# Three joints of a seven-product trunk put into written order, and a kernel's last loads reordered

## The chip, the cores and the metric

One core of one Trainium2 chip runs the whole program, in one launch. The time is device microseconds (us) of that core, the median of the runs; lower is better. The engines are named as the profile names them: PE (TensorE, matmuls), PEld (its weight loads), DVE (VectorE), ACT (ScalarE), POOL (GpSimd), and SP (SyncE), which here only issues transfers. PE's clock has two levels, 1.2 and 2.4 GHz; the profile gives the granted share of the upper one.

## The reference

A trunk of two layers over x of 1024 positions by 1024 channels, in float32, each followed by a squared-ReLU MLP with 4096 hidden channels. Cut to what matters here:

```python
# layer 0: chunked spatial gating (SGU)
z = gelu(rmsnorm(x, g) @ w_in + b_in);  u, v = split(z)          # 2 x 2048 channels
v = layernorm(v);  s = einsum('gij,bnjgc->bnigc', w_s * mask, v) + b_s
x = x + (u * s) @ w_out
x = x + square(relu(rmsnorm(x, g) @ ffn_w1[0])) @ ffn_w2[0]      # 1024 -> 4096 -> 1024
# layer 1: RWKV-7 time mixing, then
x = x + y @ w_o
x = x + square(relu(rmsnorm(x, g) @ ffn_w1[1])) @ ffn_w2[1]
out = rmsnorm(x, final_norm_g)
```

## The kernel before, in words

Every float32 operand is split into a high part, cast to fp32r by ACT, and a low part, the rest, subtracted by DVE or POOL (`tt`, L327). Each product is three matmuls (high-high L160, low-high L161, high-low L162), each of 128 x 128 weights by 512 columns.

**Seven-product stages.** The gate's product x @ w_in[:, :2048] with its w_out, and the two MLPs, are made by `two_products` (L425). It cuts each matrix product into 2 x 2 blocks and computes it with seven block products M1 to M7 instead of eight. The left sides are A11, A12, A22 and the sums S1 to S4; the right sides are B11 to B22 and sums T1 to T4, which POOL makes (`weights`, L460). The first half, the *ups*, runs over pairs p of 128-column blocks of w1 and over M1, M5, M6, M2, M7, M3, M4 in each; one such product is 12 matmuls. `prepare(n)` (L487) loads, sums, casts and splits the weights of product n, six products ahead; `evict` (L540) turns the PSUM banks upa to upd into blocks y0 to y3, squares them and stores them to DRAM (zd). The second half, the *down* (from L612), computes these blocks times w2, in chains of 12 matmuls into banks dnu, dnv, dnw, in the order M1, M5, M6, M7, M4, M3, M2, four chains q to a step, and DVE adds each chain to the residual tiles xd0 to xd7. A *unit* u is half a step's operands: a stored block zr and a weight block w2B, each cast by ACT and split by DVE into the four tiles op... (`prepare_z` L685, `prepare_w` L697). `LAST_UNITS` (L624) says in which memory the last six units lie.

**Norm between stages.** `Spread` (L334) takes each finished residual tile t of 128 positions: `scale` (L360) squares and sums it on ACT, takes a root on ACT (rs), refines the reciprocal root on DVE (five small instructions, L243 to L252), and DVE scales it (sn, L368). `transpose` (L370) makes eight PE transposes into two banks st, and from them the split parts of A22 and S1 (t below 4), or of A11, A12, S2, S3 and S4 (t from 4 on). So a full set of left sides stands only after the last tile. There are two of these, f0 behind the gate's down and f1 behind the rwkv's last product wo.

**What sets the order.** A scheduler orders the instructions of PE, DVE, ACT and POOL by its own estimates, except inside `tc.manual_schedule`, where the named engines keep the written order: the last 14 products of the ups and the down up to its last three steps (L772). Each engine then runs its list strictly in order, and SP issues transfers in order on one queue. The rwkv part in between is not touched.

Three kinds of joint come up below: into the ups of a stage (the gate's behind the v products, the MLPs' behind the gate's down and behind wo), and from the ups to the down of the same stage (in all three stages).

Of the kernel before, what the change touches and what calls it, by code (L numbers as in the profile page):

```python
# [12 lines left out]
F32 = mybir.dt.float32  # L13
# [108 lines left out]
def trunk(ctx: ExitStack, tc: tile.TileContext, a: dict, out: bass.AP):  # L122
# [211 lines left out]
    class Spread:  # L334


        def __init__(self, xs, g, tag, lag):
            self.xs, self.tag, self.lag = xs, tag, lag
# [4 lines left out]
            self.side, self.raw, self.wait = {}, [], []  # L343
            self.spilled = [dq.tile([P, 1024], F32, name=f"xm{tag}_{t}") for t in range(NT)]

        def open(self, name, where):
# [8 lines left out]
        def put(self, name, q, x, eng):  # L355
            hi, lo = [v[:, :, q * P : (q + 1) * P] for v in self.side[name]]
# [13 lines left out]
        def transpose(self, t):  # L370
            xn, q = self.xns[t % 3], t % 4
            o = []
            for j in range(2):
                o.append(pt(f"st{t}{j}_{self.tag}").rearrange("p (k n) -> p k n", k=4))
# [4 lines left out]
            if t < 4:  # L379
                if t == 0:  # L380
                    self.open("A22", 0)
                    self.open("S1", 1)
# [6 lines left out]
            else:  # L389
                if t == 4:  # L390
                    self.open("A11", (0, 1))
                    self.open("A12", (2, 3))
                    self.open("S2", 2)
                    self.open("S3", 3)
                    self.open("S4", (6, 7))
# [18 lines left out]
        def tick(self):  # L414
            for w in self.wait:
                w[1] += 1
            if self.wait and self.wait[0][1] >= self.lag:
                self.transpose(self.wait.pop(0)[0])
# [6 lines left out]
    def two_products(i, sides, w1, w2, residual, after_factory, gate=None):  # L425
# [9 lines left out]

        def load_pair(p):
            tags = (("raw0", "raw1"), ("wh0", "wl0"))[p % 2]
# [14 lines left out]
        if gate:  # L452
            gate.ws = ta[:, HB:].rearrange("p (s e i) -> p s e i", s=2, e=2)
            gate.open(0)
# [29 lines left out]
        ring = ("wh1", "wl1", "wh3", "wl3", "wh2", "wl2")  # L484
# [55 lines left out]
        def evict(m, p):  # L540

            if not ys:
                ys.extend(xt(j, f"y{j}_{i}").rearrange("p (e n) -> p e n", e=2) for j in range(4))
                u12.extend(tp.tile([P, HB], F32, tag=t, name=f"{t}_{i}") for t in ("tu", "td"))
            y1, y2, s13, s24 = ys
            u1, u2 = u12
            todo, held[:] = list(held), []
# [19 lines left out]
            if m == "M1":  # L567
                nc.scalar.copy(out=u1, in_=bank("a", p))
                if gate:
                    gate.open(p + 1)  # L570
# [9 lines left out]
            elif m == "M7":  # L580
# [8 lines left out]
                if gate:  # L589
                    gate.mix(p, "C22", s13[:, 1])  # L590
# [30 lines left out]
        raws, w12 = ("raw0", "raw1", "wh0", "wl0"), ("wh1", "wl1", "wh2", "wl2")  # L621
        if gate:
            UNITS = [raws, "h2", "h3", w12, "h1", "h0"]
            LAST_UNITS = ["h0", "h1", "h2", ("z2", "z3"), "h3", ("z6", "z7")]  # L624
        else:
            UNITS = [raws, "h2", "h1", "h3", "h0", w12]
            LAST_UNITS = ["h1", "h3", ("z2", "z3"), ("wh3", "wl3", "wh2", "wl2"), "h2", ("ta", "tb", "wh1", "wl1")]
# [45 lines left out]
        def side_b(u):  # L673

            gr, m = steps[u // 2]
            b = {kind: wr[gr, kind][:, 2 * (u % 2) : 2 * (u % 2) + 2] for kind in ("B11", "B12", "B21", "B22")}
# [62 lines left out]
        def up(first, last):  # L739
            for n in range(first, last):  # L740
# [4 lines left out]
                if early and 1 <= n <= 2:  # L745
                    sides.flush()
                for w in meanwhile.get(n - len(seq), ()):
# [6 lines left out]
        if gate:  # L754
            meanwhile = {
                -6: [lambda: load_z(0), lambda: load_z(1), lambda: load_w(0, ("B11", "B12"))],
                -5: [lambda: load_w(0, ("B22", "B21"))],
# [3 lines left out]
        else:  # L761
# [3 lines left out]
                -4: [lambda: load_w(0, ("B22", "B21")), lambda: unit(0)],  # L765
                -3: [lambda: unit(1)],
            }
        for n in range(6):
            prepare(n)
        ready = len(seq) - 14  # L770
        up(0, ready)
        with tc.manual_schedule(engines={ET.PE, ET.DVE, ET.Activation, ET.SP}):  # L772
# [3 lines left out]
            load_x(range(4))  # L776
            load_w(1, ("B12", "B11"))
            unit(2)
            unit(3)
            for n in range(len(steps) - 3):  # L780
                for q in range(4):
# [3 lines left out]
                    out()  # L785
# [6 lines left out]
        for q in range(4):  # L792
            chain(n, q)()
            (prepare_w if q % 2 else prepare_z)(2 * n + q // 2 + 4)
            after(q)
            tick()
        for q in range(4):
            chain(n + 1, q)()
            tick()
            if hasattr(after, "half"):  # L800
                after.half(4 + q)
            chain(n + 2, q)()
            after(4 + q)
            tick()
        return xs


    def sgu(norm, x, load_x, after_factory):
# [26 lines left out]
        st = sp.tile([P, NT, 8, 6], F32, name="vstat", bufs=1)  # L835

# [96 lines left out]


# [43 lines left out]
        with tc.manual_schedule(engines={ET.PE, ET.DVE, ET.Activation, ET.SP}):  # L978
            for c in range(2, 8):
# [5 lines left out]
                for t in range(NT):  # L985
# [3 lines left out]
                    if t > 1:  # L989
                        v_stat(c, t - 2)  # L990
                    if 0 < t < 3 and c < 7:
                        stream.ahead()
                    if sums and t > 4:
                        sums.pop(0)()
                    if (c, t) == (2, 2):
# [19 lines left out]

        mv = sp.tile([P, NT, 2], F32, name="vmv", bufs=1)
        for t in range(NT):
            nc.vector.bn_aggr(out=mv[:, t, :], in_=st[:, t, :, :])
        rstd = sp.tile([P, NT], F32, name="vrstd", bufs=1)
        nmr = sp.tile([P, NT], F32, name="vnmr", bufs=1)  # L1020
        nc.scalar.activation(out=rstd, in_=mv[:, :, 1], func=AF.Sqrt, bias=eps_t[LN_EPS])
        rstd = rsqrt_refine(rstd, mv[:, :, 1], NT, "v", 1.0, LN_EPS)
        nc.vector.scalar_tensor_tensor(
            out=nmr, in0=mv[:, :, 0], scalar=-1.0, in1=rstd, op0=ALU.mult, op1=ALU.mult
        )

        sums_close()

        class Gate:


            def __init__(self):
                self.v, self.taken = {}, {}

            def open(self, p):
                if p >= E // 256:
                    return
                if not p:
                    self.mixing(0)
                vt = self.v[p] = [  # L1040
                    xt(4 + 2 * (p % 2) + hf, f"vn{p}{hf}").rearrange("p (n c) -> p n c", n=4) for hf in range(2)
                ]
                for hf in range(2):
# [1139 lines left out]
```

## Time and profile before

| | us |
|---|---|
| runs (three) | 2683.47, 2692.83, 2696.07 |
| median | 2692.83 |
| profiled execution | 2697.68 |
| its span, first to last instruction | 2696.0 |
| mean granted PE clock | 0.979 |
| PE busy / DVE / ACT / POOL | 2563.1 / 1976.7 / 1049.8 / 720.4 |

The stages stand in the span at about: norm and v products 0 to 206, the gate's ups 206 to 403 and down 403 to 547, the MLP 0 ups 547 to 931 and down to 1155, rwkv to 1980, wo to 2051, the MLP 1 ups 2051 to 2386 and down to 2686. Busy time is a mean over all of these. In a fully used stretch of 50 us PE is busy for 50.00; what a joint loses is read from the gaps of PE there and from the stretch behind a gap in which the granted clock is at its lower level.

### The profile page before, as it was taken

How to read it: one execution, taken by the hardware profiler on the slowest of the kernel's cores; microseconds unless marked ns; L12 is line 12 of the kernel's file. 1: busy time of each engine (PE TensorE's matmuls, PEld its weight loads, DVE VectorE, ACT ScalarE, POOL GpSimd, SP SyncE). 2: the span in 40 equal slices, each digit the busy share in tenths (PEclk: the TensorE clock that was granted, in tenths of full speed). 3: DMA queues.
4: the chain of work that ended last, by engine and by line, in shares of the span. 5: the costliest groups of instructions: out<-in, count | busy, mean ns of one | idle time of the engine just before them, and what ended most of it. 6: DMA issues, size and time to landing. Idle time of an engine off the chain costs nothing. (4 is left out here: it accounts for less than half of the span.)

```text
span 2696.0 us, 41800 instructions
## 1 busy us (share of the span) xinstructions
PE 2563.1 (95%) x16202; PEld 2169.1 (80%) x16202; DVE 1976.7 (73%) x3011; ACT 1049.8 (39%) x1725; POOL 720.4 (27%) x545
## 2 busy tenths in 40 slices
PE   8999998989999999999999999977898999999998
PEld 8997887868888788877677898967877888878887
DVE  6448768787766887776676547999688766687777
ACT  4235434353333433345553322324425333343334
POOL 2243210143332000013464413244425333200002
PEclk9999999999999999999999999989899999999999
DMA  5424557335443744333577854444743644384332
GB/s 192 169 94 142 175 202 260 111 114 188 152 149 129 283 157 141 125 117 94 178 175 179 212 157 119 115 97 102 193 157 113 201 139 160 117 299 154 129 125 94
DMA packets 342616, 418.71 MB, mean 155 GB/s; under 512 B 91561, under 2 KB 238097, under 8 KB 342417
## 3 DMA queue, kind: packets, MB, share of 16 engines
q1 hardware_dynamic: 340208, 409.41, 48.5%
q0 software_dynamic: 2064, 6.36, 0.7%
q8 instruction: 127, 2.08, 0.3%
q14 instruction: 73, 0.59, 0.1%
q10 hardware_dynamic: 144, 0.26, 0.0%
HBM read 277.48 MB, written 138.48 MB: 154 GB/s over the span
## 5 line engine op out<-in xcount | busy, mean ns | idle before, releaser
L327 DVE TENSOR_TENSOR w1s<-w1r,w1s 128x512 fp32r<-128x512 f32 x120 | 128.5, 1072 | 72.1 <-ACT w1s L331 71.8
L161 PE MATMUL dnu<-oph 128*128 128x512 f32 x416 | 162.8, 391 | 0.9 <-DVE oph L327 0.9
L160 PE MATMUL dnu<-oph 128*128 128x512 f32 x416 | 163.6, 393 | 0.0
L162 PE MATMUL dnu<-oph 128*128 128x512 f32 x416 | 163.3, 392 | 0.0
L327 DVE TENSOR_TENSOR xd<-xd,dnu 128x512 f32<-128x512 f32 x160 | 109.3, 683 | 63.6 <-PE dnu L162 63.4
L327 POOL TENSOR_TENSOR ta<-w1r 128x512 f32<-128x512 f32 x40 | 57.7, 1443 | 365.3 <-DMA w1r<-in_ffn_w_dram 311.4
L693 ACT CAST oph<-w2B 128x1024 fp32r<-128x1024 f32 x90 | 94.4, 1049 | 154.4 <-DVE w2B L327 148.9
L160 PE MATMUL v<-whs,ht_n 128*128 128x256 f32 x512 | 146.6, 286 | 0.2 <-ACT ht_n L306 0.2
L162 PE MATMUL v<-whs,ht_n 128*128 128x256 f32 x512 | 144.3, 282 | 0.2 <-DVE ht_n L165 0.2
L691 ACT CAST oph<-zr 128x1024 fp32r<-128x1024 f32 x89 | 93.2, 1048 | 130.1 <-issue 78.6
L161 PE MATMUL v<-wls,ht_n 128*128 128x256 f32 x512 | 143.8, 281 | 0.0
L331 ACT CAST w1s<-w1r 128x512 fp32r<-128x512 f32 x120 | 74.1, 618 | 124.1 <-PE upa L162 61.5
L327 DVE TENSOR_TENSOR oph<-w2B,oph 128x1024 fp32r<-128x1024 f32 x90 | 109.6, 1218 | 0.0
L327 DVE TENSOR_TENSOR oph<-zr,oph 128x1024 fp32r<-128x1024 f32 x89 | 108.4, 1218 | 0.6 <-ACT oph L691 0.6
L331 ACT CAST w1s<-tb 128x512 fp32r<-128x512 f32 x78 | 48.4, 620 | 144.1 <-PE upb L162 65.2
L160 PE MATMUL p<-xs,whs 128*128 128x512 f32 x256 | 103.8, 405 | 0.1
L77 DVE TENSOR_TENSOR wls<-raw,whs 128x1024 fp32r<-128x1024 f32 x52 | 73.7, 1419 | 40.8 <-ACT whs L76 40.3
L162 PE MATMUL p<-xs,wls 128*128 128x512 f32 x256 | 101.5, 397 | 1.1 <-DVE wls L77 1.1
L161 PE MATMUL p<-xs,whs 128*128 128x512 f32 x256 | 101.6, 397 | 0.9 <-DVE xs L1175 0.9
L162 PE MATMUL upc<-sS_f,w1s 128*128 128x512 f32 x256 | 101.2, 396 | 0.9 <-DVE w1s L327 0.9
L327 DVE TENSOR_TENSOR y<-y,y 128x512 f32<-128x512 f32 x152 | 100.0, 683 | 2.0 <-ACT y L1077 0.7
L161 PE MATMUL upa<-sS_f,w1s 128*128 128x512 f32 x256 | 101.2, 395 | 0.2 <-POOL sS_f L327 0.2
(702 smaller groups left out, 8209.5 us busy)
## 6 DMA issues: line engine op xcount, KB each, us to landing
w1r<-in_ffn_w_dram SPq DMA_DIRECT2D x64, 512.0 KB, 4.3
w2B<-in_ffn_w_dram SPq DMA_DIRECT2D x64, 512.0 KB, 5.0
raw<-in_rwkv_w_rkv_dram SPq DMA_DIRECT2D x32, 512.0 KB, 4.8
arp<-ar_d SPq DMA_DIRECT2D x62, 256.0 KB, 5.0
raw<-in_sgu_w_in_dram SPq DMA_DIRECT2D x16, 512.0 KB, 4.6
vd<-v SPq DMA_DIRECT2D x16, 512.0 KB, 3.4
vn<-vd SPq DMA_DIRECT2D x16, 512.0 KB, 4.7
w1r<-in_sgu_w_in_dram SPq DMA_DIRECT2D x16, 512.0 KB, 4.3
```

The source lines that it names most:

```text
L77: (low or nc.vector).tensor_tensor(out=wl, in0=raw, in1=wh.bitcast(F32), op=ALU.subtract)
L160: nc.tensor.matmul(o, sh, mh, start=first, stop=False, skip_group_check=more)
L161: nc.tensor.matmul(o, sh, ml, start=False, stop=False, skip_group_check=more)
L162: nc.tensor.matmul(o, sl, mh, start=False, stop=last, skip_group_check=more)
L327: eng.tensor_tensor(out=out, in0=x, in1=y, op=op)
L331: nc.scalar.copy(out=dst[:, 0], in_=x)
L691: nc.scalar.copy(out=four[0], in_=z)
L693: nc.scalar.copy(out=four[2], in_=b)
```

## The change

**Joints into the ups.** `two_products` becomes a generator with `yield`s, so that the stage before can start its first `prepare` calls at a chosen place. Behind the v products the ups' first part now stands inside `manual_schedule` for PE, DVE and ACT, and so do wo's last tiles (t from 4 on) and the last three steps of the down ahead of the MLP. `Spread.scale` is split: the part on ACT comes first, and the reciprocal root and the scaling (`rest`) come behind the next transposes. Its parts S2 (t < 7), S3 and S4 are kept raw (`owed`) and split later (`release`), S4's sum in tiles sm instead of the tile td; for f1 the A12 part of t = 4 to 6 is also copied raw by ACT. f0's transposes use the banks of pool pb. In the gate bn_aggr is done tile by tile, the split of S4 (`sums_close`) comes behind the second product, and the scaling of the next pair's v comes at M7.

**Joints from the ups to the down.** The loads of xd0 to xd3, of B21 of the first quarter and of B12 and B11 of the second stand behind the first chains, so that the blocks zr that come next are issued ahead of them. The additions of M5's chains are written one chain later.

**Memory.** The ring of weight slots is turned, the second MLP swaps wh0/wl0 with wh2/wl2, and the gate's last units lie elsewhere.

```diff
+        def release(self, *names):
+            for n in names:
+                for w in self.owed.pop(n, ()):
+                    self.put(n, *w)
         def scale(self, t):
             ...
-            ri = rsqrt_refine(rs, ss, 1, "n")
-            nc.vector.scalar_tensor_tensor(out=xn, in0=x, scalar=ri, in1=self.gbc, op0=ALU.mult, op1=ALU.mult)
+            self.roots.append((t, rs, ss))
+        def rest(self):
+            while self.roots:
+                t, rs, ss = self.roots.pop(0)
+                ri = rsqrt_refine(rs, ss, 1, "n")
+                nc.vector.scalar_tensor_tensor(
+                    out=self.xns[t % 3], in0=self.xs[t], scalar=ri, in1=self.gbc, op0=ALU.mult, op1=ALU.mult
+                )
...
             else:
-                raw = self.raw[q]
-                s4 = tp.tile([P, HB], F32, tag="td", name=f"s4{q}_{self.tag}").rearrange("p (k n) -> p k n", k=4)
+                raw, late = self.raw[q], t < NT - 1
+                more = xt(t, f"sm{q}_{self.tag}").rearrange("p (i k n) -> p i k n", i=2, k=4)
                 self.put("A11", q, o[0], v)
+                tt(v, raw[:, 1], raw[:, 1], o[0], ALU.subtract)
+                if late and self.full:
+                    nc.scalar.copy(out=more[:, 1], in_=o[1])
+                    self.owed.setdefault("A12", []).append((q, more[:, 1], v))
+                if not late:
+                    self.put("S2", q, raw[:, 1], g)
+                if not (late and self.full):
+                    self.put("A12", q, o[1], v)
+                tt(v, more[:, 0], raw[:, 1], o[1], ALU.add)
                 tt(v, raw[:, 0], o[0], raw[:, 0], ALU.subtract)
-                tt(v, raw[:, 1], raw[:, 1], o[0], ALU.subtract)
-                self.put("A12", q, o[1], v)
-                tt(v, s4, raw[:, 1], o[1], ALU.add)
-                self.put("S2", q, raw[:, 1], g)
-                self.put("S3", q, raw[:, 0], g)
-                self.put("S4", q, s4, g)
+                for n, x in (("S2", raw[:, 1]), ("S3", raw[:, 0]), ("S4", more[:, 0])):
+                    if late or n != "S2":
+                        self.owed.setdefault(n, []).append((q, x, g))
...
-        ring = ("wh1", "wl1", "wh3", "wl3", "wh2", "wl2")
+        ring = ("wh3", "wl3", f"wh{s2}", f"wl{s2}", "wh1", "wl1")
+        if gate:
+            ring = ring[4:] + ring[:4]
...
-            LAST_UNITS = ["h0", "h1", "h2", ("z2", "z3"), "h3", ("z6", "z7")]
+            LAST_UNITS = [("wh3", "wl3", "ta", "tb"), ("z2", "z3"), "h2", ("z6", "z7"), "h3", w12]
...
+                if early and n < 5:
+                    sides.release(*(("S2", "S4") if sides.side.get("S4") else ("S2",), ("A12",), (), ("S3",), ("S4",))[n])
...
-                -4: [lambda: load_w(0, ("B22", "B21")), lambda: unit(0)],
+                -4: [lambda: load_w(0, ("B22",)), lambda: unit(0)],
...
-        up(0, ready)
+        with tc.manual_schedule(engines={ET.PE, ET.DVE, ET.Activation}):
+            up(0, ready)
         with tc.manual_schedule(engines={ET.PE, ET.DVE, ET.Activation, ET.SP}):
             up(ready, len(seq))
             ...
-            load_x(range(4))
-            load_w(1, ("B12", "B11"))
             unit(2)
             unit(3)
+            owed = []
             for n in range(len(steps) - 3):
                 for q in range(4):
                     out = chain(n, q)
                     ...
-                    out()
+                    if n == 0 and q < 3:
+                        (lambda: load_x(range(4)), lambda: load_w(0, ("B21",)), lambda: load_w(1, ("B12", "B11")))[q]()
+                    if n == 1:
+                        owed.append(out)
+                    else:
+                        out()
+                        if owed:
+                            owed.pop(0)()
...
+        with tc.manual_schedule(engines={ET.PE, ET.DVE, ET.Activation}) if following else ExitStack():
+            for q in range(4):
+                chain(n, q)()
+                ...
+                after(q)
+                tick()
+            for q in range(4):
+                chain(n + 1, q)()
+                tick()
+                if following and q == 3:
+                    next(following)
+                    after.release("S2", "S4")
+                ...
+                chain(n + 2, q)()
+                after(4 + q)
+                tick()
+                if following and q == 2:
+                    next(following)
```

SP's list at the gate's joint from ups to down, before. The names: zd2_3S3 and zd2_3S4 are blocks stored by the ups; xd0 to xd3 are the residual tiles; w2B121 and w2B111 weight blocks of the second quarter; zr1 and zr0 hold the stored blocks that come back (S3 for step M6, A22 for M7, S4 next).

```order

```

The same place of SP's list in the changed kernel.

```order

```

The first three block loads now stand ahead of xd0 to xd3 and of all weight blocks there; w2B210 (B21 of the first quarter) moved in from an earlier place.

DVE's list at the gate's end, before, from the transposes of tile 4 on. xd5 to xd7 are the residual tiles, dnv and dnw the banks of the down's last two steps, st40 to st51 the transposed tiles 4 and 5, sA111 and sA121 the low parts of A11 and A12, ri_n, rm_n and rq_n the refining of the reciprocal root.

```order

```

The same for the changed kernel, from the addition of tile 6 on; sm1 is the raw sum for S4, sn4_f0 the scaled tile.

```order

```

Before, the parts of tiles 4 and 5 stand mixed between additions and the steps of another tile's root. Now each tile is a block: both additions of the next tile, the five parts of this one, the root's five steps, the scaling.

DVE's list where the gate's first weights are split, before. w1s0 to w1s5 are the split weights of the ups' products in order (w1s0 is M1's), v6 and v7 the last v tiles, vstat their statistics, sS23 a low part of S2.

```order

```

The same for the changed kernel: what stands around w1s0 there.

```order

```

w1s0 stood ahead of v7's first bias and now stands behind its last, and behind w1s5 and w1s3.

## Rows read from the trace of the kernel before

**Rows 1.** The page's first part: busy us, share, instructions.

```profile
PE 2563.1 (95%) x16202; PEld 2169.1 (80%) x16202; DVE 1976.7 (73%) x3011; ACT 1049.8 (39%) x1725; POOL 720.4 (27%) x545
```

**Rows 2.** Busy time by window: PE, PEld, DVE, ACT, POOL (instructions), clock, DMA share, GB/s.

```profile
200.00:250.00 50.00, 43.53 (x229) 36.97 (x228) 40.10 (x67) 25.49 (x45) 19.42 (x12) 0.93 0.40 123
...
550.00:600.00 50.00, 40.67 (x198) 32.09 (x199) 42.90 (x76) 27.58 (x52) 21.66 (x18) 0.93 0.28 98
...
2050.00:2100.00 50.00, 43.25 (x182) 33.62 (x181) 40.47 (x57) 23.25 (x42) 31.34 (x23) 0.93 0.42 141
```

**Rows 3.** Waits of PE, 205 to 245 us: total, times, longest.

```profile
PE s0C L1068 <- issue: 3.4, 1, 3.4
PE upa L160 <- ACT tu L568: 1.9, 1, 1.9
```

**Rows 4.** DVE's timeline there: start, us, instruction [idle before].

```profile
205.92 1.33 DVE L327 TENSOR_TENSOR w1s<-w1r,w1s 128x512 fp32r<-128x512 f32 x1 [0.31 <-ACT w1s L331]
...
208.67 0.67 DVE L327 TENSOR_TENSOR sS<-tbs,sS 128x512 fp32r<-128x512 f32 x1
```

**Rows 5.** PE's timeline at the gate's joint to the down.

```profile
443.00 0.77 PE L160 MATMUL dnu<-op6wh,op6raw 128*128 128x512 f32 x1 [6.42 <-DVE xd L327]
...
448.18 0.39 PE L160 MATMUL dnu<-op6wh,op6raw 128*128 128x512 f32 x1
```

**Rows 6.** Timeline of SP and ACT there.

```profile
407.39 3.48 SPq L522 DMA_DIRECT2D zd_3S<-y  x4
...
420.98 0.73 SPq L645 DMA_DIRECT2D zr<-zd_0S  x1
...
430.75 1.05 ACT L691 CAST op6raw<-zr 128x1024 fp32r<-128x1024 f32 x1 [8.31 <-DMA zr<-zd_0S]
```

**Rows 7.** The chain that ended last, at MLP 1's joint to the down: start, us, what.

```profile
2387.65 10.73 DMA zr<-zd_0S
...
2411.50 0.43 PE dnu L161
...
2414.62 0.23 PE dnu L160
```

**Rows 8.** Waits of PE, 928 to 940 and 2400 to 2416 us.

```profile
PE dnu L160 <- DVE xd L327: 1.8, 1, 1.8
...
PE dnu L160 <- DVE xd L327: 2.4, 1, 2.4
```

**Rows 9.** Waits of PE, 530 to 615 us.

```profile
PE st_f L377 <- DVE xd L327: 5.8, 1, 5.8
```

**Rows 10.** Timeline of DVE, ACT and POOL behind the gate's down.

```profile
545.49 0.16 DVE L243 RECIPROCAL ri_n<-rs 128x1 f32<-128x1 f32 x1 [0.42 <-ACT rs L366]
...
548.77 2.33 DVE L368 SCALAR_TENSOR_TENSOR sn_f<-xd,ri_n,sn_f 128x1024 f32<-128x1024 f32 x1
...
558.34 0.69 DVE L327 TENSOR_TENSOR sA_f<-st_f,sA_f 128x512 fp32r<-128x512 f32 x1 [4.14 <-ACT sA_f L357]
558.94 0.68 DVE L327 TENSOR_TENSOR sr_f<-sr_f,st_f 128x512 f32<-128x512 f32 x1
...
591.21 1.29 DVE L368 SCALAR_TENSOR_TENSOR sn_f<-xd,ri_n,sn_f 128x1024 f32<-128x1024 f32 x1
548.76 1.25 POOL L327 TENSOR_TENSOR ta<-w1r 128x512 f32<-128x512 f32 x1 [12.82 <-DVE ri_n L252]
...
558.20 1.07 ACT L364 ACTIVATE sn_f<-xd 128x1024 f32<-128x1024 f32 x1
...
559.65 0.62 ACT L357 CAST sS_f<-sr_f 128x512 fp32r<-128x512 f32 x1
```

**Rows 11.** PE's timeline in wo's last tiles.

```profile
2034.98 1.07 PE L377 MATMUL st_f<-ident,sn_f 128*128 128x128 f32 x8 [0.48 <-DVE sn_f L368]
```

**Rows 12.** Timeline of POOL and DVE there.

```profile
2051.99 1.40 POOL L327 TENSOR_TENSOR ta<-w1r 128x512 f32<-128x512 f32 x1 [10.50 <-DMA w1r<-in_ffn_w_dram]
...
2062.24 0.69 DVE L327 TENSOR_TENSOR s_f<-sr_f,st_f 128x512 f32<-128x512 f32 x1 [4.68 <-POOL sS_f L327]
```

More of the change, by code (lines that the diff above doesn't have):

```diff
@@ L342, in __init__, with open @@
             nc.gpsimd.dma_start(out=self.gbc, in_=g.partition_broadcast(P))
-            self.side, self.raw, self.wait = {}, [], []
+            self.side, self.raw, self.wait, self.roots, self.next, self.owed = {}, [], [], [], None, {}
             self.spilled = [dq.tile([P, 1024], F32, name=f"xm{tag}_{t}") for t in range(NT)]
-        def open(self, name, where):
+        HOME = {"A22": 0, "S1": 1, "A11": (0, 1), "A12": (2, 3), "S2": 2, "S3": 3, "S4": (6, 7)}
+        def open(self, name):
+            where = self.HOME[name]
             if isinstance(where, tuple):
@@ L355, in put @@
         def put(self, name, q, x, eng):
+            if name not in self.side:
+                self.open(name)
             hi, lo = [v[:, :, q * P : (q + 1) * P] for v in self.side[name]]
@@ L569, in evict @@
                 if gate:
-                    gate.open(p + 1)
+                    gate.load(p + 1)
             elif m == "M6":
@@ L791, in two_products, with finish @@
         tick = getattr(after, "tick", lambda: None)
[L792 to L804, printed above, removed]
-        return xs
+        following = getattr(after, "next", None)
+        with tc.manual_schedule(engines={ET.PE, ET.DVE, ET.Activation}) if following else ExitStack():
+            for q in range(4):
+                chain(n, q)()
+                u = 2 * n + 4
+                if following:
+                    for f in ((lambda: prepare_z(u),), (lambda: prepare_w(u), lambda: prepare_z(u + 1)), (lambda: prepare_w(u + 1),), ())[q]:
+                        f()
+                else:
+                    (prepare_w if q % 2 else prepare_z)(u + q // 2)
+                after(q)
[6 more added lines that the diff above has]
+                    after.release("S2", "S4")
+                if hasattr(after, "half"):
+                    after.half(4 + q)
+                chain(n + 2, q)()
[3 more added lines that the diff above has]
+                    next(following)
+        return xs
+    def finish(product):
+        while True:
+            try:
+                next(product)
+            except StopIteration as e:
+                return e.value
     def sgu(norm, x, load_x, after_factory):
@@ L935, in sgu @@
+        gate = Gate()
+        gate.close = sums_close
+        product = two_products(
+            2, type("Sides", (), {"side": side}), w_in[:, :E], w_out, lambda t: x_in[t * P : (t + 1) * P, :],
+            after_factory, gate,
+        )
         for c in range(2):
@@ L994, in sgu @@
                         sums.pop(0)()
+                    if (c, t) == (7, NT - 1):
+                        next(product)
                     if (c, t) == (2, 2):
@@ L1014, in sgu @@
                     v_stat(c, t)
[L1016 to L1025, printed above, removed]
@@ L1079, in sgu @@
-        gate = Gate()
-        sides = type("Sides", (), {"side": side})
-        return two_products(
-            2, sides, w_in[:, :E], w_out, lambda t: x_in[t * P : (t + 1) * P, :], after_factory, gate,
-        )
+            gate.load(0)
+            gate.mixing(0)
+            for n in range(2):
+                next(product)
+            for t in range(NT - 2, NT):
+                nc.vector.bn_aggr(out=mv[:, t, :], in_=st[:, t, :, :])
+            rstd = sp.tile([P, NT], F32, name="vrstd", bufs=1)
@@ L1086, in trunk @@
+            nmr = sp.tile([P, NT], F32, name="vnmr", bufs=1)
+            nc.scalar.activation(out=rstd, in_=mv[:, :, 1], func=AF.Sqrt, bias=eps_t[LN_EPS])
+            rstd = rsqrt_refine(rstd, mv[:, :, 1], NT, "v", 1.0, LN_EPS)
+            nc.vector.scalar_tensor_tensor(
+                out=nmr, in0=mv[:, :, 0], scalar=-1.0, in1=rstd, op0=ALU.mult, op1=ALU.mult
+            )
+            gate.norm = rstd, nmr
+            gate.scale(0)
+        return finish(product)
     KAPPA = float(np.exp(-0.5))
@@ L2018, in rwkv @@
         product(3, wo[3], range(4), xs)
-        for t in range(4, NT):
-            product(2, wo[2], [t], xz)
-            product(3, wo[3], [t], xs)
+        with tc.manual_schedule(engines={ET.PE, ET.DVE, ET.Activation}):
+            for t in range(4, NT):
+                product(2, wo[2], [t], xz)
+                if t == NT - 1:
+                    next(after.next)
+                product(3, wo[3], [t], xs)
+                if t == NT - 2:
+                    next(after.next)
         return xs
```

152 lines of the change are left out of this document (79 added, 73 removed).

## The prediction

> **What bounds the kernel now.** I read the page first: PE is busy for 2563.1 of the 2696 us [rows 1], so at most about 130 us can be won by any change of order. Next I read busy time by windows of 50 us, to find where the missing time lies. The reader is to see that it lies at the joints: PE was busy for 43.53 of 50 us behind the v products, 40.67 behind the gate's down and 43.25 behind wo, each with a granted clock of 0.93 [rows 2]. A clock of 0.93 over 50 us is at most 3.5 us more lost, since 7% of the upper level was not granted. So the three joints into the ups lost at most 6.5 + 3.5 = 10.0, 9.3 + 3.5 = 12.8 and 6.75 + 3.5 = 10.3 us. Then I read PE's waits. At the gate's joint to its down PE waited 6.42 us for one addition of DVE, and its matmuls were slow from 443.0 to 448.2 [rows 5]. At the slow level one takes 0.43 us from start to start, else 0.23 [rows 7]; half of 5.2 us is 2.5 more, so 8.9. The same joint of MLP 0 waited 1.8 and that of MLP 1 2.4 [rows 8], the latter with slow matmuls from its restart to some time between 2411.5 and 2414.6 [rows 7], estimated at 1.7: 4.1. All six together are some 48 us. That is the ceiling, since nothing else is moved.
>
> **Joints to the down: gain.** The wait of 6.42 us on an addition is not the cause. DVE's list stood behind the split of S3's block, whose cast on ACT had waited 8.31 us for its load; that load was issued at 420.98 and used at 430.75 [rows 6]. MLP 1 shows the same: its load of S3 took from 2387.65 for 10.73 us [rows 7]. In SP's list the load stood behind xd0 to xd3 and two weight blocks; now it stands directly behind the last stores. The last of those were issued from 407.39 for 3.48 us, so it can be issued at about 411, some 10 us earlier; by then DVE has also split S1's first block, which holds the same slot. PE reached the end of its ready work at 443.00 − 6.42 = 436.6; the operands were 6.4 late, and 10 earlier covers that. What comes late next is xd0 to xd3 and B21, pushed back by three block loads and by waits for zr slots (SP stands in order behind them). Eight transfers of 512 KB stood in front of S3's first (four of xd, two each of the two weight blocks), and it came 9.8 us after its issue [rows 6], so one costs an estimated 1.1; three more in front are 3.3 us, with the waits for slots some 5. The pushed blocks are used by the first additions and, B21, only by step M4; I take that as hidden. Gain: 8.9 + 1.8 + 4.1 = 14.8 us, nothing if the pushed blocks are late by as much, more than that never. M5's later additions cost the same instructions, so nothing.
>
> The trace shows landing about 10 us after issue while others are in flight. The Trainium skill ("DMA: Bandwidth & Descriptors", section "Queues, rings and completion order") says that descriptors are consumed in ring order but that completion is not first in, first out per issuing engine. By the first half the reorder gives the 14.8, by the second part of it could be lost. The rows agree with the first half.
>
> **Joint behind the gate's down (f0).** Before, PE waited 5.8 us in one piece [rows 9], and DVE stood idle for 4.14 us behind a cast of ACT, which itself followed PE's transposes [rows 10]. The scheduler's mixing is gone. In the written order each tile from t = 4 on is one serial turn. Two additions of DVE take 0.60 each from start to start (558.34 to 558.94), ACT's square, its sum and root 1.45 (558.20 to 559.65), the cast of A11 behind these as long as the 0.62 of another cast of that shape: together 3.3. Then DVE has five parts at 0.60, 3.0; five small instructions at 0.16, 0.8; and the scaling, 1.2 of its 1.29 [all rows 10]. That is 8.3 us a turn. PE has in a turn 24 matmuls of 0.23 [rows 7] and eight transposes, 1.07 [rows 11]: 6.6. So PE stalls 1.7 in each of three turns, 5.1. Behind these, seven low parts of weights at 0.6, 4.2, now stand in DVE's list ahead of the last tile's root, with the two additions and five parts; tile 7's scaling then ends about 4 us later than its 592.4 of before (591.21 with 1.2, [rows 10]). PE covers some of that with its ready M5 and M4 products. On POOL a weight sum that waits for a load stands ahead of S3's parts, an estimated 1.2. Walking the list so, the second pair's M1 starts about 3 us later than before: +3. Bounds: −9, when the turns overlap better than that and half of the 12.8 and more comes back; +10, when each of POOL's parts also holds DVE.
>
> Of that second bound the trace shows a case: DVE's scaling took 2.33 instead of 1.29 when POOL's sum ran beside it, from 548.76 for 1.25 [rows 10]. The Trainium skill ("SBUF — State Buffer", section "Who interferes with whom") has it as a lock: a DVE instruction with two SBUF inputs and a GpSimd instruction that reads SBUF shut each other out. By it the postponed S2, S3 and S4 parts, now run beside the splits of weights, hold one DVE instruction each; the walk without it gives +3, with it up to +10.
>
> **Joint behind wo (f1).** The turn here has four additions in place of two, +1.2, and one part fewer, since A12 is only copied, −0.6, and its ACT copy adds about 0.2: 9.1. PE's 6.6 is the same, so two turns lose 2.5 each and the third some 3, 8 in all. Against that two waits go: POOL stood 10.50 us for a weight load, and DVE 4.68 behind POOL [rows 12]; the loads of the second pair now go into slots that are free earlier. The joint lost at most 10.3. Walking it gives the second pair's M1 5 us later than before: +5, bounds −9 and +10 for the same reasons as above.
>
> **Joint behind the v products.** PE waited 3.4 for the mixing of the gate, which needs the layer norm's root, and 1.9 for the eviction of the first product [rows 3]. In the written order the root's small instructions stand together, ahead of S4's splits, which takes most of the 3.4. But w1s0, which M1's third matmul needs, now stands behind w1s5, a bias, w1s3 and sS23: before, that stretch went from 205.92 to 209.34 [rows 4], so w1s0, ready ahead of it then, is ready at about 210. PE begins these ups at about 206.6 and has two matmuls that don't need the low part, so it waits an estimated 2.7 that it did not wait before. And the mixing's result stands behind both splits of S4, each of 1024 elements, so M2's bank is late by about 2. I take −1, bounds −7 and +5.
>
> **Rest.** The steady ups keep PE full, and the rwkv part and the end are not moved: 0. The turned ring and the other homes move no instruction outside the joints; three ACT copies of 0.6 are hidden by ACT's idle time.
>
> **Sum.** −14.8 + 3 + 5 − 1 = −7.8 us. From the profiled execution's 2697.68 that is 2689.9; the median is 4.85 below that execution, so 2685.0 by the median of the runs.
>
> **Rivals.** A: the joints do overlap as written. What the walks take as serial (DVE's parts wait for a cast behind the square) is partly hidden, as in three of the tiles before; the idle 4.14 and 4.68 us of DVE are then gone and no waits take their place. J by J: f0 −6, f1 −5, v −4, downs −14.8, together −30: 2663. For it speaks that 5.8 of f0's 9.3 us stood in one wait [rows 9]; against it that DVE was busy for 42.9 of 50 us there [rows 2], so it is nearly the bound itself.
> B, the other side: DVE and POOL hold each other at the new places. From some eight held instructions of 1.2 a joint on, f0 and f1 cost +10 each and the v joint +5, and the downs give only 8, because pushed blocks come late: +17, 2710. For it speak the row of 2.33 and a POOL that is busy for 31.34 of 50 us behind wo [rows 2]; against it that POOL's parts are as many as before.
> C: the reordered loads do not land earlier, since transfers in flight share the engines and S3's stores were not the only thing it stood behind. Then the downs give nothing, and the sum is +7: 2700.
>
> **How the numbers follow.** What a measurement of this kernel can tell from no change is about 0.5%, 13.5 us: below 2679.4 is faster, above 2706.3 slower. The forecast, −7.8 with its own range of 2673 to 2697, has 0.48; about a sixth of it lies below 2679. A has 0.30, C 0.08, B 0.14. Faster: 0.30 + 0.08 = 0.38. Slower: B and a little of C, 0.15. Within: 0.47. The range reaches from A's 2663, with 3 below for the full bounds, to 2708 of B's 2710: 2660 to 2708.
>
> **What would show it.** Right: no wait of PE on an addition at 436 us or at its two counterparts, the S3 load issued near 411, and the clock there at its upper level; behind the gate's down gaps of PE of 1 to 2 us ahead of each of st50, st60 and st70 for a late scaling, with DVE waiting for a cast of sA; behind wo the same with 2 to 3; PE waiting about 2.7 for w1s0 at 207. Wrong: PE's gaps in 550 to 600 and 2050 to 2100 below 4 us (A); DVE instructions of 1.9 to 2.4 in rows at both (B); the S3 cast still waiting for its load (C).

## The result: 1% slower, the gain at three joints lost at two others

The changed kernel takes 2718.8 us (median of the runs beside it) where the kernel before takes 2692.3: ratio 1.0100, interval 1.0075 to 1.0124. The forecast was 2685 with a range of 2660 to 2708; the time lies above the range. One of the changed kernel's six executions took 7235.3 us; it is left out of the ratio, and without it the median is 2717.6.

A shift table tells where it went. It is read from PE's timelines of the two profiled executions: the time of the first matmul of each stage's down, of the first matmul into bank dnw (the last step of the down's first quarter), and of the first transpose of f1. The shift of such a point against before, less that of the point ahead of it, is what the stretch between them costs. The spans differ by 19.0 us and the medians by 26.5, since the profiled execution of before was 5.4 above its median here and that of the change 2.0 below.

| stretch | forecast | measured |
|---|---|---|
| to the gate's down (the joint behind v) | −1 | −0.1 |
| the gate's down (joint from its ups) | −8.9 | −9.0 |
| behind the gate's down, f0, to MLP 0's down | +3 | +20.2 |
| MLP 0's down | −1.8 | −2.1 |
| rwkv and wo to f1's first transpose | 0 | −0.8 |
| behind wo, f1, to MLP 1's down | +5 | +15.9 |
| MLP 1's down | −4.1 | −4.3 |
| the rest | 0 | −0.7 |
| sum (spans 2696.0 and 2715.0) | −7.8 | +19.0 |

So the three joints to the down came out within 0.3 us, and the two into the MLPs' ups cost 36 us instead of 8. The busy time by windows, columns as in [rows 2]: first two windows where it gained, of the kernel before and then of the changed one; then the changed kernel's two windows where it lost, which answer to lines of [rows 2].

```profile
400.00:450.00 50.00, 42.60 (x173) 33.89 (x172) 42.93 (x48) 22.39 (x24) 0.00 (x0) 0.93 0.83 312
2400.00:2450.00 50.00, 47.58 (x202) 38.92 (x201) 42.39 (x47) 21.10 (x22) 0.00 (x0) 0.97 0.56 192
```

```profile
400.00:450.00 50.00, 49.02 (x213) 39.65 (x212) 48.68 (x54) 26.87 (x28) 0.00 (x0) 1.00 0.97 359
2400.00:2450.00 50.00, 50.00 (x221) 41.24 (x220) 49.04 (x54) 23.81 (x25) 0.00 (x0) 1.00 0.84 309
```

```profile
550.00:600.00 50.00, 37.30 (x157) 28.84 (x156) 38.22 (x65) 22.31 (x44) 14.32 (x11) 0.90 0.24 84
2050.00:2100.00 50.00, 38.42 (x159) 30.00 (x158) 37.45 (x62) 22.68 (x44) 17.89 (x13) 0.90 0.18 63
```

The reader is to see two things. At the joints to the down PE is full or nearly so, and its clock is at the upper level. At the other two every engine is less busy than in [rows 2], DVE and POOL too: no engine is full there, and what PE waits for has to be read from its waits. And the granted clock fell from 0.93 to 0.90. PE's waits from 515 to 625 us, which answer to [rows 9], and then those behind wo, from 2000 to 2130 us (the longest of each):

```profile
PE st_f L396 <- DVE sn_f L385: 11.4, 7, 4.7
PE st_f L396 <- DVE xd L327: 6.7, 1, 6.7
PE dnw L160 <- ACT sr_f L401: 1.3, 1, 1.3
PE upc L160 <- DVE sm_f L327: 1.3, 1, 1.3
```

```profile
PE st_f L396 <- DVE sn_f L385: 10.8, 4, 3.7
PE upc L161 <- POOL sS_f L327: 2.3, 1, 2.3
PE upc L162 <- DVE w1s L327: 2.2, 1, 2.2
```

PE waited 22.8 us in all at the gate's end, against 11.0 before. That is 12 of the 20.2. The other 8 are clock, an estimate: by windows of 100 us the granted clock was 0.91 and 0.98 from 500 to 700 us, against 0.97 and 1.00 before, 6 and 2 us. Behind wo it is the same with some 10 (17.9 against 8.1) and 6 (0.93 and 0.98 from 2000 to 2200 us, against 0.97 and 1.00).

### The profile page after: what moved, and what is told of

Read it like the earlier page. It is cut to its first block, busy times and chain, and to the rows that moved or that the text cites. A ratio compares the mean times of both kernels' runs of the same rounds, so it can differ in the third digit from the quotient of the medians.

```text
span 2715.0 us, 41844 instructions
## 1 busy us (share of the span) xinstructions
PE 2571.3 (95%) x16202; PEld 2172.9 (80%) x16202; DVE 1981.2 (73%) x3011; ACT 1048.0 (39%) x1728; POOL 699.3 (26%) x545
## 5 line engine op out<-in xcount | busy, mean ns | idle before, releaser
L161 PE MATMUL dnu<-oph 128*128 128x512 f32 x400 | 155.9, 390 | 0.9 <-DVE oph L327 0.9
L162 PE MATMUL dnu<-oph 128*128 128x512 f32 x400 | 156.6, 392 | 0.0
L160 PE MATMUL dnu<-oph 128*128 128x512 f32 x400 | 156.6, 391 | 0.0
L327 DVE TENSOR_TENSOR w1s<-w1r,w1s 128x512 fp32r<-128x512 f32 x120 | 108.5, 904 | 25.3 <-ACT w1s L331 25.2
L162 PE MATMUL upc<-sS_f,w1s 128*128 128x512 f32 x256 | 104.0, 406 | 2.8 <-DVE w1s L327 2.8
L160 PE MATMUL upc<-sS_f,w1s 128*128 128x512 f32 x256 | 104.1, 407 | 1.4 <-DVE sm_f L327 1.3
L161 PE MATMUL upc<-sS_f,w1s 128*128 128x512 f32 x256 | 102.9, 402 | 2.3 <-POOL sS_f L327 2.3
L544 DVE SCALAR_TENSOR_TENSOR y<-y 128x512 f32<-128x512 f32 x100 | 100.8, 1011 | 3.3
```

What stands on the lines that cost most here:

```text
L160: nc.tensor.matmul(o, sh, mh, start=first, stop=False, skip_group_check=more)
L161: nc.tensor.matmul(o, sh, ml, start=False, stop=False, skip_group_check=more)
L162: nc.tensor.matmul(o, sl, mh, start=False, stop=last, skip_group_check=more)
L327: eng.tensor_tensor(out=out, in0=x, in1=y, op=op)
L544: eng.scalar_tensor_tensor(out=q, in0=q, scalar=0.0, in1=q, op0=ALU.max, op1=MUL)
```

## The three joints that gained

SP's and ACT's timeline at the gate's joint, against [rows 6]. First the two lines of the kernel before that stood between the stores and the load, then the changed kernel:

```profile
415.00 2.85 SPq L737 DMA_DIRECT2D xd<-in_x_dram  x4
417.90 2.98 SPq L639 DMA_DIRECT2D w2B<-in_sgu_w_out_dram  x4
```

```profile
410.85 0.32 SPq L672 DMA_DIRECT2D zr<-zd_0S  x1
414.33 0.32 SPq L672 DMA_DIRECT2D zr<-zd_1S  x1
...
418.23 2.26 SPq L764 DMA_DIRECT2D xd<-in_x_dram  x4
...
422.25 1.04 ACT L718 CAST op6raw<-zr 128x1024 fp32r<-128x1024 f32 x1
```

The load of S3's block is issued at 410.85 (forecast 411, before 420.98) and its cast, at 422.25 instead of 430.75, has no wait ahead of it. PE's wait of 6.42 us for an addition is gone, and so are those of 1.8 and 2.4 at the other two joints. To see what this part does by itself, the kernel before got it alone.

```diff
-            load_x(range(4))
-            load_w(1, ("B12", "B11"))
             unit(2)
             unit(3)
...
+                    if n == 0 and q < 3:
+                        (lambda: load_x(range(4)), lambda: load_w(0, ("B21",)), lambda: load_w(1, ("B12", "B11")))[q]()
+                    if n == 1:
+                        owed.append(out)      # M5's additions one chain later
...
```

> The kernel before with one part of the change alone: the loads of xd0 to xd3, B21 and the second quarter's B12/B11 behind the first chains of the down, and M5's additions one chain later. Shifts against before read from the changed kernel's trace: joints to the down -9.0, -1.4 and -4.3, joints into the ups +19.5 and +15.9. If these parts are independent, this kernel keeps only the first three: about 2692 - 14.7 = 2677 to 2678, and the three waits of PE on an addition (6.4, 1.8, 2.4) are gone. Rival: the gain in the changed kernel came from its other memory homes or from the shifted joint ahead; then less than half of it shows, 2685 or more.

Measured: 2684.7 us, ratio 0.9955 (0.9942 to 0.9967) against before's 2695.0 beside it. Shifts −9.0, −2.1, −4.3 at the three joints, +0.4 and 0.0 at the two joints into the MLPs' ups. The three joints gain the same without the rest of the change, so the rival (memory homes) falls by the shifts. By the median it would not: that is 7 us above the number expected, next to the rival's 2685, in part since before's own median was 3 higher beside it. The runs show a gain of 10 to 12, the spans 13.0. Then without M5's part:

```diff
-                    if n == 1:
-                        owed.append(out)
-                    else:
-                        out()
-                        if owed:
-                            owed.pop(0)()
+                    out()
```

> The kernel before with the reordered loads alone, M5's additions at their old place. By the prediction's step the loads give all of the gain and M5's later additions nothing: the same as with both, 2684 to 2685, joints to the down shorter by 9.0, 2.0 and 4.3. Rival: the hold of M5's additions is what brings the split of S3's block to the front of DVE's list; then the waits come back in part, 2688 to 2692.

Measured: 2683.5 us, ratio 0.9951 (0.9939 to 0.9963). Shifts −8.3, −2.1, −4.3; PE still waits 0.4 us at the gate's joint. So the loads bring nearly all, and the later additions some 0.6 at the gate's joint and nothing at the other two, too little to show in the time. This kernel and the one ahead of it are the fastest of the study, and nothing tells them apart.

## The two joints that lost: whose written order it is

First the written order was taken from the two joints and from the MLPs' ups behind them (up to their last 14 products), with everything else left; then from ACT alone, then from DVE and ACT. The edit is the same in three places, of which one is shown.

```diff
-        with tc.manual_schedule(engines={ET.PE, ET.DVE, ET.Activation}):
+        with ExitStack():          # scheduled; in the next two: {ET.PE, ET.DVE}, {ET.PE}
```

> The changed kernel without the written order at the two joints into the MLPs' ups (the scheduler orders PE, DVE and ACT there again; homes, raw copies, postponed parts and the reordered loads stay). Theory W, the written order itself costs the 35 us: the joints return to about before's, 2692 - 15 = 2677, at most 2685. Rival M, the postponed parts and the weight sums that POOL now starts later (their tiles ta and tb hold an operand of the gate's last units) cost it: the time stays at 2705 or more, with POOL's sums still beside the second tile's root at the gate's end.

> The changed kernel with PE and DVE in the written order at the two joints into the MLPs' ups, but ACT ordered by the scheduler there. Theory A (ACT's written list costs most of the 35 us): 2700 or less. Rival D (DVE's written list, a tile as one block with the root behind its parts, costs most): 2712 or more.

> The changed kernel with PE alone in the written order at the two joints; ACT and DVE are ordered by the scheduler there. If PE's order costs nothing, this runs as the kernel with all three engines scheduled, 2692. If PE's order (transposes at fixed places between chains) is what makes the joints long, 2710 or more.

| written at f0 and f1 | us | ratio (interval) | f0 | f1 |
|---|---|---|---|---|
| PE, DVE, ACT (the change) | 2718.8 | 1.0100 (1.0075 to 1.0124) | +20.2 | +15.9 |
| PE, DVE | 2707.5 | 1.0042 (1.0026 to 1.0059) | +12.3 | +10.2 |
| PE | 2699.2 | 1.0014 (1.0003 to 1.0026) | +8.5 | +10.2 |
| none | 2691.6 | 0.9978 (0.9968 to 0.9988) | +3.2 | +2.7 |

The postponed parts, raw copies and new homes (the tiles' other places in memory) alone cost about 3 us a joint; the written order costs the other 17 and 13. With none written I had expected 2677 and at most 2685. The 2691.6 is above that: 3 us stayed at each joint, and two other stretches, to the gate's down and to f1, took 2.2 and 2.4 us longer in this execution. Taken off in this order, ACT's list is worth 7.9 and 5.7 us, DVE's 3.8 and 0, PE's 5.3 and 7.5. Neither of the two expectations for ACT alone (2700 or less, 2712 or more) was met: the time lies between them. PE's order by itself I had expected at nothing or at all of it.

What ACT's list does is seen in one turn of the norm, tile 3 at the gate's end of the changed kernel. DVE's timeline, then ACT's and POOL's:

```profile
548.23 2.40 DVE L385 SCALAR_TENSOR_TENSOR sn_f<-xd,ri_n,sn_f 128x1024 f32<-128x1024 f32 x1
550.55 0.67 DVE L327 TENSOR_TENSOR xd<-xd,dnu 128x512 f32<-128x512 f32 x1
553.72 0.69 DVE L327 TENSOR_TENSOR sA_f<-st_f,sA_f 128x512 fp32r<-128x512 f32 x1 [2.50 <-ACT sA_f L362]
...
555.70 2.40 DVE L385 SCALAR_TENSOR_TENSOR sn_f<-xd,ri_n,sn_f 128x1024 f32<-128x1024 f32 x1
```

```profile
551.26 1.06 ACT L375 ACTIVATE sn_f<-xd 128x1024 f32<-128x1024 f32 x1 [3.07 <-DVE xd L327]
552.22 0.18 ACT L375 ACTIVATION_READ_ACCUMULATOR sn_f<-xd 128x1 f32 x1
552.44 0.29 ACT L377 ACTIVATE rs<-ss,eps 128x1 f32<-128x1 f32 x1
552.64 0.56 ACT L401 COPY sr_f<-st_f 128x512 f32<-128x512 f32 x1
553.11 0.59 ACT L362 CAST sA_f<-st_f 128x512 fp32r<-128x512 f32 x1
```

```profile
548.26 1.29 POOL L327 TENSOR_TENSOR sS_f<-sr_f,sS_f 128x512 fp32r<-128x512 f32 x1 [6.20 <-ACT sS_f L362]
555.74 1.28 POOL L327 TENSOR_TENSOR sS_f<-sr_f,sS_f 128x512 fp32r<-128x512 f32 x1 [6.19 <-ACT sS_f L362]
```

DVE ends its addition at 551.2; ACT then squares the next tile, takes the root, and only then copies and casts the transposes, which PE had ended at 551.9; DVE stands 2.50 us. And as the same list releases POOL's part of S1 at the same place in each of these turns, it meets DVE's scaling three times in a row: 2.40 instead of 1.28. This turn is 7.5 us, and PE's own work in it, 12 matmuls of 0.23 and eight transposes in 1.07, is 3.8. Two experiments are to take these apart, the second effect first: S1's split a turn later.

```diff
-                self.put("S1", q, raw[:, 1], g)
+                self.owed.setdefault("S1", []).append((q, raw[:, 1], g))
...   (in tick, ahead of the transposes)
+            self.release("S1")
```

> The changed kernel with one thing moved: the split of S1 (ACT's cast, POOL's low part) of a tile is written ahead of the next tile's transposes, behind that tile's square, instead of directly behind its own subtraction. Theory L, DVE's scaling is held by POOL's S1 part because both start together every turn (2.40 in place of 1.28 us, three times at the gate's end and once behind wo): the scaling takes 1.3 and the joints shorten by about 1.1 less ACT's 0.5 each, 2 to 4 us in all, to about 2715. Rival: the hold only fills time in which DVE would wait for ACT's cast anyway (it waits 2.0 to 2.5 us there); then 2718 to 2719, within 1 us of the changed kernel.

Measured: 2720.6 us, ratio 1.0088 (1.0075 to 1.0102); joints +19.3 and +17.9. No gain, as the rival has it, but the test is weaker than planned: of three held scalings behind the second tile one was freed (1.29), two met the next part of POOL (2.40, 2.38), and the waits for a cast grew from 2.50 to 3.02. It shows that POOL's part can't be moved by half a turn for a profit here, not what the hold costs. Now ACT's casts ahead of the next square, in their own turn; the split of S1 stays a turn later in this edit, now behind the next tile's transposes:

```diff
-                self.put("S1", q, raw[:, 1], g)
+                self.owed.setdefault("S1", []).append((q, raw[:, 1], g))
...
         def __call__(self, t):
-            self.scale(t)
+            self.square = t
...   (in tick, behind the transposes and the previous tile's S1)
+            if self.square is not None:
+                self.scale(self.square)
+                self.square = None
```

> The changed kernel with ACT's written order of a turn of the norm altered alone: the copy and casts of a tile's transposes (and the cast of the previous tile's S1) stand ahead of the next tile's square and root, not behind them. Theory A, the turn is too long because DVE waits 2.0 to 2.5 us in each for a cast that stands behind a square on ACT: the five waits at the gate's end and three behind wo fall to below 1, the joints into the ups shorten by about 8 and 5 us, and the time is 2704 to 2709 against the changed kernel's 2719. Rival T, the late sums of POOL and the casts of the weights that wait for them set the joint's end: the gain is spent waiting there, at most 3 us, 2716 or more.

Measured: 2699.2 us, ratio 1.0016 (1.0006 to 1.0026); joints +8.3 and +8.2, so 11.9 and 7.7 of the loss came back, more than expected. DVE's waits from 515 to 625 us, of the changed kernel and of this one:

```profile
DVE sA_f L327 <- ACT sA_f L362: 12.3, 7, 2.5
```

```profile
DVE sA_f L327 <- ACT sA_f L363: 2.1, 4, 1.2
```

This is the largest single cause, and it needed no engine to work less: the same casts and squares, swapped in one list. The two effects are not quite apart at the gate's end, since two scalings that POOL's part of S1 had held went from 2.40 and 2.41 to 1.28 there, so up to 2.2 of the 11.9 may be the hold. Behind wo one scaling was held in either kernel (2.42, then 2.24), and 7.7 came back all the same.

## The other part: POOL's sums and the block of weights

[rows 12] had shown POOL waiting for a load ahead of parts that others needed. In the changed kernel POOL is still ordered by the scheduler while ACT and DVE are fixed. At the gate's end its five weight sums run beside the second tile's root and scaling; the DVE rows there:

```profile
538.34 1.18 DVE L251 SCALAR_TENSOR_TENSOR rq_n<-rq_n,rm_n 128x1 f32<-128x1 f32 x1
539.56 1.18 DVE L252 SCALAR_TENSOR_TENSOR ri_n<-rq_n,ri_n 128x1 f32<-128x1 f32 x1
540.78 2.37 DVE L385 SCALAR_TENSOR_TENSOR sn_f<-xd,ri_n,sn_f 128x1024 f32<-128x1024 f32 x1
```

```profile
535.66 1.41 POOL L327 TENSOR_TENSOR tb<-w1r,w1r 128x512 f32<-128x512 f32 x1 [13.63 <-PE dnu L161]
...
540.80 1.26 POOL L327 TENSOR_TENSOR te<-tb,w1r 128x512 f32<-128x512 f32 x1
```

A root step on a single column, 0.16 us alone, took 1.18, and ended with a POOL sum each time; PE waited its 6.68 behind this. The sums begin at 535.66 because tb now holds an operand of one of the gate's last units (before, they ran from 526.90). So POOL was put into the written order too:

```diff
-        with tc.manual_schedule(engines={ET.PE, ET.DVE, ET.Activation}):
+        with tc.manual_schedule(engines={ET.PE, ET.DVE, ET.Activation, ET.Pool}):
```

> The changed kernel with POOL in the written order too at the two joints into the MLPs' ups, so that its weight sums stand behind S1's parts and behind the parts of S2 written before them, and pair 2's sums behind S3 and S4. Theory P, POOL's list (ordered by the scheduler) is what holds the written lists of ACT and DVE: five sums beside the second tile's root at the gate's end (sn 2.37 and three root steps of about 1.2 in place of 0.16, a wait of 6.68 of PE), ACT's cast of w1s3 waiting 6.8 and 8.0 us for POOL's te, S3 waiting 2.3: gain 8 to 15 us in all, 2704 to 2711. Rival: the sums are only moved and hold the first weights' casts instead, so no gain, 2715 to 2725.

Measured: 2711.5 us, ratio 1.0054 (1.0040 to 1.0067); joints +14.7 and +11.1, so 5.5 and 4.8 back. The time is half a us above the range expected, and well below the rival's. The wait of 6.68 fell to 3.04, and ACT's waits for POOL did not go away: 8.4 us for te at the gate's end, 6.8 without this edit.

All together, with S2's and S4's early splits left to the later place:

> Three edits on the changed kernel together: ACT's casts ahead of the next square, POOL in the written order too, and the early splits of S2 and S4 ahead of the gate's last chain left to the later place. By theories A and P the gains add: 8 us of POOL's order, 13 of the casts, and the burst of four parts that held tile 6's root and scaling for 3 us goes: 2719 - 8 - 13 - 3 = 2695, which would be near the kernel before, with its joints still some 8 us behind. If the end of the joint is set by the last tile's block of weights, 2703 or more.

```diff
-                    next(following)
-                    after.release("S2", "S4")
+                    next(following)
```

Measured: 2690.5 us, ratio 0.9982 (0.9973 to 0.9991); joints +4.2 and +3.3. So 16.0 and 12.6 came back, where the casts and POOL's order by themselves gave 17.4 and 12.5: the gains add nearly in full. What the late S2 and S4 give was not run alone. One long wait of PE was left at the gate's end, ahead of the last tile's transposes. PE's row and DVE's list ahead of it, in this kernel:

```profile
587.87 1.97 PE L397 MATMUL st_f<-ident,sn_f 128*128 128x128 f32 x8 [5.55 <-DVE sn_f L386]
```

```profile
579.60 0.16 DVE L243 RECIPROCAL ri_n<-rs 128x1 f32<-128x1 f32 x1
579.67 0.14 DVE L244 TENSOR_SCALAR rm_n<-ss 128x1 f32<-128x1 f32 x1
579.72 1.65 DVE L327 TENSOR_TENSOR w1s<-te,w1s 128x512 fp32r<-128x512 f32 x1
581.30 1.24 DVE L250 TENSOR_TENSOR rq_n<-ri_n 128x1 f32<-128x1 f32 x1
582.46 0.68 DVE L327 TENSOR_TENSOR w1s<-w1r,w1s 128x512 fp32r<-128x512 f32 x1
583.07 1.21 DVE L251 SCALAR_TENSOR_TENSOR rq_n<-rq_n,rm_n 128x1 f32<-128x1 f32 x1
```

The splits of later weights stand between the root's steps. In the code these steps are one piece. The splits come from behind the block of written order: by the code, three of the four belong to products four to six, which are prepared outside of any block, and one to the block that follows; the scheduler wove them in. The last experiment prepares the first six products inside the block, and writes the last tile's root and scaling ahead of the third and the later ones:

```diff
+            self.rest()
             if t == NT - 2:
-                next(self.next)
-            self.rest()
+                for _ in range(4):
+                    next(self.next)
...   (in two_products)
-            if n < 3:
+            if n < 3 or not gate:
                 yield
```

> The kernel with ACT's casts ahead, POOL in written order and the late S2 and S4, plus one more edit: the last tile's root and scaling are written ahead of the splits of the products' weights from the third on, and these stand in the same block of written order (before, four of them had moved in between from the following block). Theory B, the last wait of 5.55 us at the gate's end and its like behind wo come from that block of splits ahead of the root: the waits ahead of the last tile's transposes fall below 2, the two joints gain about 4 us each, 2690.5 - 8 = 2682 to 2684, below the kernel with the loads alone. Rival: the splits are only late now and M5's and M4's second products wait for them; 2688 or more.

Measured: 2687.7 us, ratio 0.9968 (0.9956 to 0.9980); joints +1.3 and +3.2. Expected were 2682 to 2684, and 2688 or more by the rival. At the gate's end the wait is gone and 2.9 came back; behind wo nothing: there it turned into waits for weights, as the rival has it (2.8 us for one split). So 20.2 and 15.9 are brought down to 1.3 and 3.2 step by step, and what is left is no better than the old scheduled joints. The loads alone stay the better version.

## Why the prediction was wrong

**The joints to the down were right**, in size and in mechanism: the load behind eight transfers, 10 us earlier, the pushed blocks hidden. That M5's later additions give nothing was nearly so (0.6 us in the trace). The Trainium skill ("DMA: Bandwidth & Descriptors", "Queues, rings and completion order") has descriptors consumed in ring order, and the rows agree: the load issued 10.1 us earlier was cast 8.5 us earlier. Of its other half, completion out of that order, no run here shows a case.

**The joint behind v** was right in its waits: 3.2 us for w1s0 (forecast 2.7) and 3.4 for M2's bank behind S4's splits (forecast about 2), in place of [rows 3]. Its sum of −0.1 in this one execution is luck. The eight other kernels with the same code there have +0.6 to +3.2, seven of them +2.2 or more, and the two with before's code have +0.1 and −2.4: the joint more likely costs some 2 us than gains 1.

**The step that failed is the walk of the two joints into the MLPs' ups**, +3 and +5, where +20.2 and +15.9 were measured. The chain in its turn was right, and most of the gaps of PE that it named came near: 1.6, 4.7 and 1.7 us ahead of tiles 5, 6 and 7 (forecast 1 to 2), behind wo 1.9, 3.7 and 3.0 (forecast 2 to 3). The turn of 8.3 us was met where nothing held DVE: the scalings of tiles 4 to 6 ended at 567.4, 575.6 and 587.0, turns of 8.2 and 11.4, with 9.3 ahead; a POOL instruction held the scaling in the longer two (2.41, 2.28). What was missing is seen in PE's rows at the gate's end, ahead of the transposes of tiles 1, 3, 4, 5 and 6:

```profile
543.80 1.11 PE L396 MATMUL st_f<-ident,sn_f 128*128 128x128 f32 x4 [6.68 <-DVE xd L327]
...
558.25 1.37 PE L396 MATMUL st_f<-ident,sn_f 128*128 128x128 f32 x8 [1.94 <-DVE sn_f L385]
...
567.44 1.10 PE L396 MATMUL st_f<-ident,sn_f 128*128 128x128 f32 x8 [1.01 <-DVE sn_f L385]
...
575.71 1.09 PE L396 MATMUL st_f<-ident,sn_f 128*128 128x128 f32 x8 [1.62 <-DVE sn_f L385]
...
587.08 1.97 PE L396 MATMUL st_f<-ident,sn_f 128*128 128x128 f32 x8 [4.73 <-DVE sn_f L385]
```

- It used that turn from tile 4 on only, and put the tiles before at nothing. The same serial chain (addition, square, cast) stood in the turns of tiles 1 to 3 too, and a POOL instruction held each scaling (2.37, 2.40, 2.40): 10.1, 7.5 and 7.5 us between the ends of the first four, where PE's work is 3.8. PE waited 11.1 us there, 7.4 at tiles 4 to 6 (forecast 5.1), and 4.2 behind them. Behind wo it waited 8.6 at tiles 5 to 7 (forecast 8); put at nothing were 2.3 at tile 3 and 5.9 in the first products.
- It set POOL's hold on DVE as a bound of +10, which the forecast did not take. The written order can make such meetings regular: a part that is released at a fixed place of one list meets the same instruction of another turn after turn. This counts at the gate's end alone: five of eight scalings and seven steps of the root were held there, before two and four. Behind wo one scaling and three steps were held, before and after alike, so the hold can hardly explain the 15.9. The Trainium skill's lock ("SBUF — State Buffer", "Who interferes with whom") agrees with the rows: sn at 548.23 went on until 1.1 us behind POOL's end at 549.55, near its own time of 1.28. With the full +10 at either joint the sum would have been nearer, yet not enough.
- It priced each matmul at the upper clock. The slower matmuls behind the added waits cost 8 and 6 us more: 14 of the 36 us.

Rival B, with a chance of 0.14, named the right side and one of the causes. That its 17 us lies near the 19.0 is luck: its +10 a joint is too small, its gain at the joints to the down too (8 for 15), and its sign, held DVE instructions in the rows at both joints, came at one. Rival A spoke of overlap that the written lists took away.

## What to carry to other kernels

Before several engines are put into a written order, walk one turn of the loop over all of their lists at once: an instruction on an engine that is little used (a square on ACT, 1.45 us with its root) becomes the bound as soon as it stands ahead of one that another engine waits for. Begin with the first turn, not where the work is largest. An engine left to the scheduler beside written lists has to be walked too, and what is written behind a block can be woven into it. Where a change has a part whose gain is worked out from a single late transfer and a part whose gain rests on overlap, measure the first alone; here it was worth some 12 us, and two of the other joints cost 36.

## Not expected of the hardware

A DVE instruction on one column of 128 partitions, 0.16 us alone, takes 1.18 to 1.25 beside a POOL sum: the hold lasts as long as POOL's instruction, not in proportion to DVE's. In these rows it strikes the root's three steps that combine two operands. The two steps ahead of them, with one each, kept their time beside POOL: 0.17 and 0.13 at 537.46 and 537.54 of the changed kernel, where POOL's sums ran from 537.03 to 539.50. What the postponed parts, raw copies and new homes cost (3 us a joint with all engines scheduled) was not taken apart, and stays open.
